# Norm and gate of the delta rule's outputs for both token tiles ahead of one pause, then all transposes

## The chip, the cores and the metric

The kernel runs on one core of one Trainium2 chip. The metric is the device time of one execution in microseconds (us). The profiler also records one execution as a trace; its times below are given from the start of the profiled span. Engines: PE multiplies and transposes, with its weight loads (PEld) beside it; DVE is the vector engine, ACT the scalar engine, POOL is GpSimd, and SP issues most of the transfers.

## The reference, cut to what matters

The layer is a normed mixer with two branches over 256 tokens of width 2048. Both branches read one combined projection of the normed input. Branch A is a gated delta rule with 8 heads of 128, branch B a causal attention with 8 heads of 128. Each branch is gated with a SiLU path, projected to 2048 and merged with sigmoid gates; then come the output projection, a norm and the residual. The change concerns the end of branch A:

```python
def step(state, inp):
    qg_i, kd_i, u_i, w_i, a_i, gl_i = inp
    v_new = u_i - jnp.einsum('bhcd,bhde->bhce', w_i, state)
    o = jnp.einsum('bhcd,bhde->bhce', qg_i, state) + jnp.einsum('bhij,bhje->bhie', a_i, v_new)
    state = state * gl_i[..., None, None] + jnp.einsum('bhcd,bhce->bhde', kd_i, v_new)
    return state, o
...
oa = gated_delta_rule(qa, ka, va, beta, g).transpose(0, 2, 1, 3)
oa = oa * lax.rsqrt(jnp.mean(oa * oa, axis=-1, keepdims=True) + NORM_EPS)
za = gdn_z.astype(jnp.float32).reshape(B, S, GDN_HEADS, GDN_HEAD_DIM)
oa = (oa * gdn_norm_w.astype(jnp.float32) * jax.nn.silu(za)).reshape(B, S, GDN_WIDTH)
u_a = oa @ w_branch_a
```

So each head's 128 outputs of a token are divided by their root mean square, multiplied by a weight and by the SiLU gate `za`, and the result enters a projection.

## The kernel before, in words

The 256 tokens are two token tiles of 128 rows (`NT` = 2). The weights stream through SBUF in blocks of 1 MB (`raw`, three buffers), and each block is split in pieces into a rounded part and the rest: ACT casts `hi` (L214) and DVE subtracts to get `lo` (L215), three buffers each. PE multiplies `hi` and `lo` with the split input `hT` in three or two matmuls per 128 rows of weight (`proj_n`, `proj_t`, all through the helper at L140). The list `ORDER` (L40) sets the order of these weight blocks: `mk0` is the first block of attention queries and keys (tiles `a_mq`, `a_mk`), after it come `mk1` and then `gb0`, the first block of the second merge gate (tile `a_gb`).

Everything else is written between those matmuls. Each side job is a Python generator in a `Queue` (L45). `tick()` (L132) is called after every fourth `hi`/`lo` pair of `proj_t` and after every six matmuls of `proj_n`; it takes 0.5 off a queue's pause, and when the pause is used up it runs the generator to its next `yield`, whose value is the new pause. The queue `gq` holds the delta rule: its scores, the triangular inverse (`inverse`, L598) and `solve` (L695). The queues `aq` hold the attention heads (`attend`, L805), one queue for even and one for odd heads. Matmuls and transposes are pinned to the order in which they are written (L137), so on PE a transpose that is not ready holds up every matmul behind it. ACT and DVE also take their instructions in order; for them a scheduler may move unpinned instructions past each other.

`solve` first forms the new values in seven steps (`sv`, L700 to L729). Then `outputs(t)` (L731) does for each token tile: the products of the two groups of four heads (`so`, L740 to L743), the squares and their sums on ACT (`jo`, L747), the factor of the norm (`fo`, L751 to L758, with a square root on ACT), and per group the gating on DVE (`os`, L763, four instructions of one head each), a pause of `OS_WAIT` = 5 (L771), four transposes on PE (`ot`, L774), and the split of the result into `oT` on ACT (L779) and DVE (L780). The tiles `os` come from the pool `wk` with two buffers under the tag "s", which the attention's scores `s` also use.

PSUM has four banks for projections (`acc`) and four for everything else (`aux`); `so`, `ot`, the attention's scores `ms`, transposed weights `pp`, products `po` and transposed results `pt` all take the latter in turn.

Two tiles reuse the buffers of the delta rule: `obT`, where the attention heads put their results, and `gb`. Whoever asks for one of them first empties the queue, so that nothing is left that still reads the old contents:

```python
def free_tile(shape, dtype, tag, name):
    gq.drain()
    return big.tile(shape, dtype, tag=tag, name=name)
```

An attention head asks for `obT` at its end (L841), after its pauses `A_WAIT2` = 6, `A_WAIT3` = 3 and `A_WAIT4` = 4 and behind its transposes `pt`. The gate `zg` of the delta rule lies in the buffer "z2", into which POOL later loads a block of the output weights (`tq`, L903). The buffers "tv" and "tw" hold the triangular inverse, and much later sums of the output product (L892).

Of the kernel before, what the change touches and what calls it, by code (L numbers as in the profile page):

```python
# [8 lines left out]
F32 = mybir.dt.float32  # L9
# [6 lines left out]
P = 128  # L16
# [16 lines left out]
OS_WAIT = 5  # L33
# [39 lines left out]
def hybrid_layer(  # L73
# [17 lines left out]
    NT = S // P  # L91
# [19 lines left out]
    big = ctx.enter_context(tc.tile_pool(name="big", bufs=1))  # L111
    wraw = ctx.enter_context(tc.tile_pool(name="wraw", bufs=3))
    wspl = ctx.enter_context(tc.tile_pool(name="wspl", bufs=3))
    wk = ctx.enter_context(tc.tile_pool(name="wk", bufs=2))
# [7 lines left out]
    def aux_tile(name):  # L122
        return aux.tile([P, 512], F32, tag="aux", name=name)
# [15 lines left out]
    def mm(*args, **kwargs):  # L139
        return pin(nc.tensor.matmul(*args, **kwargs))  # L140

    def tr(*args):
        return pin(nc.tensor.transpose(*args))
# [26 lines left out]
    ident = cst.tile([P, P], F32, name="ident")  # L170
# [298 lines left out]
    HG = H // 2  # L469
# [6 lines left out]
    def sl(h):  # L476
        return gsl[h // HG][:, h % HG, :]

    def vt(t, h):
        return gvt[h // HG][:, t, h % HG, :]  # L480
# [100 lines left out]
    def queries(p):  # L581
        h = 2 * p
        pq = proj_t(CQ + h * P, f"q{h}")
        qTs = [halves(pq[m], f"q{h + m}") for m in range(2)]
        for m in range(2):
            conv_silu(qTs[m], h + m)
        for m in range(2):
            gq.add(scores(h + m, kTs[p][m], qTs[m]))
        if p == H // 2 - 1:
            gq.add(inverse())  # L590
            gq.add(solve())
# [103 lines left out]
    def solve():  # L695
        oT = big.tile([P, H, 2 * S], F32R, tag="u1", name="oaT")
        oaT[0] = oT
        lo_, hi_ = slice(0, 64), slice(64, 128)

        def step(t, which):  # L700
            for g in range(2):
                ps = aux_tile(f"sv_{t}_{which}_{g}")
                p3 = ps.rearrange("p (h e) -> p h e", e=P)
                for hh in range(4):
                    h = g * 4 + hh
                    o_ = slice(hh * P, (hh + 1) * P)
                    if which == 0:
                        mm(ps[lo_, o_], inv[0][lo_, t, h, :], vt(t, h)[lo_], start=True, stop=True)
                    elif which == 1:
                        mm(  # L710
                            ps[hi_, o_],
                            sl(h)[lo_, t * 4 * P + 64 : t * 4 * P + 128],
                            vt(t, h)[lo_],
                            start=True,
                            stop=True,
                        )
                    elif which == 2:
                        mm(ps[hi_, o_], inv[0][hi_, t, h, :], vt(t, h)[hi_], start=True, stop=True)
                    else:
                        mm(ps[:, o_], sl(h)[:, P : 2 * P], vt(0, h), start=True, stop=True)  # L720
                v_ = gvt[g][:, t]
                if which == 0:
                    nc.scalar.copy(v_[lo_], p3[lo_])
                elif which == 1:
                    nc.vector.tensor_tensor(v_[hi_], v_[hi_], p3[hi_], op=ALU.subtract)
                elif which == 2:
                    nc.scalar.copy(v_[hi_], p3[hi_])
                else:
                    nc.vector.tensor_tensor(gvt[g][:, 1], gvt[g][:, 1], p3, op=ALU.subtract)  # L729

        def outputs(t):  # L731
            pso = []
            for g in range(2):
                ps = aux_tile(f"so_{t}_{g}")
                pso.append(ps)
                for hh in range(4):
                    h = g * 4 + hh
                    o_ = slice(hh * P, (hh + 1) * P)
                    if t == 0:
                        mm(ps[:, o_], sl(h)[:, 2 * P : 3 * P], vt(0, h), start=True, stop=True)  # L740
                    else:
                        mm(ps[:, o_], sl(h)[:, 3 * P : 4 * P], vt(0, h), start=True, stop=False)
                        mm(ps[:, o_], sl(h)[:, 5 * P : 6 * P], vt(1, h), start=False, stop=True)  # L743
                for hh in range(4):
                    h = g * 4 + hh
                    jq = wk.tile([P, P], BF16, tag="jq", name=f"jo_{t}_{h}")
                    nc.scalar.activation(  # L747
                        jq, ps[:, hh * P : (hh + 1) * P], AF.Square, accum_out=ssoo[:, t, h : h + 1]
                    )
                yield 0.5  # L750
            nc.vector.tensor_scalar(  # L751
                fo[:, t, :], ssq[:, t, :], EPS, EPS * P, op0=ALU.add, op1=ALU.mult
            )
            nc.vector.scalar_tensor_tensor(
                fo[:, t, :], ssoo[:, t, :], 1.0 / P, fo[:, t, :], op0=ALU.mult, op1=ALU.add
            )
            nc.scalar.activation(fo[:, t, :], fo[:, t, :], AF.Sqrt)
            nc.vector.reciprocal(fo[:, t, :], fo[:, t, :])  # L758
            for g in range(2):
                os_ = wk.tile([P, 4, P], F32, tag="s", name=f"os_{t}_{g}")  # L760
                for hh in range(4):
                    h = g * 4 + hh
                    nc.vector.scalar_tensor_tensor(  # L763
                        os_[:, hh, :],
                        pso[g][:, hh * P : (hh + 1) * P],
                        fo[:, t, h : h + 1],
                        zg()[:, t, h * P : (h + 1) * P],
                        op0=ALU.mult,
                        op1=ALU.mult,
                    )  # L770
                yield OS_WAIT  # L771
                pt = aux_tile(f"ot_{t}_{g}")
                for hh in range(4):
                    tr(pt[:, hh * P : (hh + 1) * P], os_[:, hh, :], ident)  # L774
                p3 = pt.rearrange("p (h n) -> p h n", n=P)
                hi = oT[:, g * 4 : g * 4 + 4, t * P : (t + 1) * P]
                lo = oT[:, g * 4 : g * 4 + 4, S + t * P : S + (t + 1) * P]
                gn = pcol[:, NTAP * NCV : NTAP * NCV + 1]
                nc.scalar.activation(hi, p3, AF.Copy, scale=gn)  # L779
                nc.vector.scalar_tensor_tensor(  # L780
                    lo, p3, gn, hi.bitcast(F32), op0=ALU.mult, op1=ALU.subtract
                )
                yield 0.5

        while vq.items or v_left[0]:
            yield 1
        for t in range(NT):
            for which in range(3):
                step(t, which)
                yield SV_WAIT  # L790
            if t == 0:
                step(0, 3)
                yield SV_WAIT
        for t in range(NT):
            yield from outputs(t)

    mv = big.tile([P, NT, GW], F32, tag="z1", name="mv")

# [320 lines left out]
```

## Time and profile before

| | before |
|---|---|
| median of 3 runs | 786.91 us (785.95 to 787.24) |
| the profiled execution | 785.26 us |
| its span, first to last instruction | 783.2 us |
| PE busy in the span | 770.5 us |
| DVE busy | 530.8 us |
| ACT busy | 412.1 us |
| mean granted TensorE clock | 0.994 |

In a line of the page or of a group, "L140 PE MATMUL so<-gdn" names the source line, the engine, the operation and the tiles written and read; a helper's line stands for all who call it, so the tiles tell which step it is. A bracket at the end of a line gives how long the engine stood idle before it and what ended that. Ends of matmuls are modelled and overlap; starts are what can be compared. An fp32 product or a chain of two counts each of its matmuls.

### The profile page before, as it was taken

What the parts mean: (1) busy time and instruction counts of PE and PEld (TensorE: products, weight loads), DVE (VectorE), ACT (ScalarE), POOL (GpSimd) and SP (SyncE); (2) the same over time, 40 slices, a digit from 0 to 9 for tenths busy, and PEclk for the clock granted to TensorE, in tenths of its full rate; (3) what the DMA queues carried; (4) which work ended last, traced back from release to release, by engine and by line L of the source; (5) the groups of instructions that cost most, each with busy time, mean ns of one, the idle gap of its engine ahead of it and who ended that gap; (6) DMA issues with size and microseconds to landing.
All of it is one profiled execution on the core that took longest, in us unless ns stands there. A gap on an engine that the chain in (4) does not pass through costs nothing.

```text
span 783.2 us, 10310 instructions
## 1 busy us (share of the span) xinstructions
PE 770.5 (98%) x3947; PEld 657.4 (84%) x3947; DVE 530.8 (68%) x876; ACT 412.1 (53%) x623; POOL 24.6 (3%) x47
## 2 busy tenths in 40 slices
PE   8999999999999999999999989999999999999996
PEld 7898988898888888888888878888888888888884
DVE  5777668887865898975444646554645668986573
ACT  5676666565554545455536546455464445465551
POOL 3000000010020000001100000000000000000000
PEclk9999999999999999999999999999999999999998
DMA  8576675466578656556833454556456555577442
GB/s 306 165 235 213 189 208 166 148 194 191 166 227 266 210 167 211 181 198 201 229 108 108 162 161 162 168 163 206 164 166 226 201 181 205 194 279 269 163 159 108
DMA packets 92823, 149.24 MB, mean 191 GB/s; under 512 B 3045, under 2 KB 46694, under 8 KB 92134
## 3 DMA queue, kind: packets, MB, share of 16 engines
q1 hardware_dynamic: 89958, 136.51, 54.1%
q0 software_dynamic: 2240, 11.02, 4.8%
q10 hardware_dynamic: 576, 1.05, 0.4%
q8 instruction: 31, 0.51, 0.3%
q14 instruction: 18, 0.15, 0.1%
HBM read 145.42 MB, written 3.15 MB: 190 GB/s over the span
## 4 chain that ended last, share of the span: by engine, by line
PE 95%; DVE 2%; ACT 2%; DMA 1%; issue 0%; SPq 0%; DVEq 0%; ACTq 0%
PE a_gb L140 11%; PE a_ga L140 11%; PE a_y L140 11%; PE a_zg L140 6%; PE a_mq L140 6%; PE a_mk L140 6%; PE a_v L140 6%; PE a_k L140 6%; PE a_zm L140 6%; PE a_mv L140 5%; PE a_ub L140 5%; PE a_ua L140 5%; PE a_q L140 4%; PE sv L140 2%; PE s L140 1%; PE so L140 1%
## 5 line engine op out<-in xcount | busy, mean ns | idle before, releaser
L140 PE MATMUL a_gb<-hi_gb,hT 128*128 128x512 f32 x256 | 83.4, 398 | 0.0
L140 PE MATMUL a_ga<-hi_ga,hT 128*128 128x512 f32 x256 | 80.8, 391 | 0.0
L215 DVE TENSOR_TENSOR lo_gb<-raw_gb,hi_gb 128x1024 fp32r<-128x1024 f32 x32 | 39.1, 1224 | 42.2 <-ACT hi_gb L214 42.2
L214 ACT CAST hi_gb<-raw_gb 128x1024 fp32r<-128x1024 f32 x32 | 33.7, 1052 | 51.2 <-PE a_gb L140 35.7
L140 PEld LDWEIGHTS a_gb<-hi_gb,hT 128*128 128x128 f32 x256 | 48.5, 189 | 10.0
L140 PEld LDWEIGHTS a_ga<-hi_ga,hT 128*128 128x128 f32 x256 | 48.1, 188 | 9.9
L214 ACT CAST hi_ga<-raw_ga 128x1024 fp32r<-128x1024 f32 x32 | 33.6, 1052 | 37.9 <-PE a_ga L140 28.0
L215 DVE TENSOR_TENSOR lo_ga<-raw_ga,hi_ga 128x1024 fp32r<-128x1024 f32 x32 | 39.1, 1223 | 16.6 <-ACT hi_ga L214 16.3
L140 PE MATMUL a_gb<-lo_gb,hT 128*128 128x512 f32 x128 | 50.1, 391 | 0.0
L140 PE MATMUL a_ga<-lo_ga,hT 128*128 128x512 f32 x128 | 49.9, 390 | 0.0
L140 PE MATMUL a_zg<-hi_zg,hT 128*128 128x348 f32 (+1 forms) x192 | 46.6, 322 | 0.0
L140 PE MATMUL a_mq<-hT,hi_mq 128*128 128x512 f32 x128 | 46.4, 405 | 0.0
L140 PE MATMUL a_mk<-hT,hi_mk 128*128 128x512 f32 x128 | 46.1, 402 | 0.0
L140 PE MATMUL a_y<-hi_y,mT 128*128 128x512 f32 x144 | 45.7, 390 | 0.0
L140 PE MATMUL a_v<-hT,hi_v 128*128 128x512 f32 x128 | 45.6, 399 | 0.0
L140 PE MATMUL a_q<-hT,hi_q 128*128 128x512 f32 x128 | 45.3, 395 | 0.0
L140 PE MATMUL a_ua<-hi_ua,oaT 128*128 128x512 f32 x128 | 41.8, 395 | 0.0
L140 PE MATMUL a_k<-hT,hi_k 128*128 128x512 f32 x128 | 40.7, 400 | 0.0
L140 PE MATMUL a_zm<-hi_zm,hT 128*128 128x512 f32 x128 | 40.6, 392 | 0.0
L140 PE MATMUL a_mv<-hi_mv,hT 128*128 128x512 f32 x128 | 40.1, 391 | 0.0
L140 PE MATMUL a_ub<-hi_ub,obT 128*128 128x512 f32 x128 | 40.1, 389 | 0.0
L140 PE MATMUL a_v<-hT,lo_v 128*128 128x256 f32 x128 | 35.9, 281 | 0.0
(318 smaller groups left out, 1909.6 us busy)
## 6 DMA issues: line engine op xcount, KB each, us to landing
raw_ga<-in_w_in_dram SPq DMA_DIRECT2D x16, 1024.0 KB, 5.1
raw_gb<-in_w_in_dram SPq DMA_DIRECT2D x16, 1024.0 KB, 5.0
raw_y<-in_w_out_dram SPq DMA_DIRECT2D x15, 1024.0 KB, 5.0
raw_q<-in_w_in_dram SPq DMA_DIRECT2D x8, 1024.0 KB, 5.5
raw_mv<-in_w_in_dram SPq DMA_DIRECT2D x8, 1024.0 KB, 5.1
raw_v<-in_w_in_dram SPq DMA_DIRECT2D x8, 1024.0 KB, 5.7
raw_zm<-in_w_in_dram SPq DMA_DIRECT2D x8, 1024.0 KB, 9.0
raw_mq<-in_w_in_dram SPq DMA_DIRECT2D x8, 1024.0 KB, 5.7
```

Source lines behind the costliest of these rows:

```text
L140: return pin(nc.tensor.matmul(*args, **kwargs))
L214: nc.scalar.copy(hi, raw)
L215: nc.vector.tensor_tensor(lo, raw, hi.bitcast(F32), op=ALU.subtract)
```

## The change

`outputs` is divided in two. `normed(t, oz)` does the products, the squares, the factor and the gating of one token tile, with a yield of 0.5 where the pause of 5 was, and writes the gated outputs into a tile `oz` of its own. `turned_outputs(t, oz)` does the transposes and the split. `solve` runs `normed` for both token tiles, then pauses once for `OS_WAIT`, then runs `turned_outputs` for both. The two `oz` tiles, 4 KB per partition each, take the buffers "tv" and "tw"; the tiles `os` are gone.

```diff
-        def outputs(t):
+        def normed(t, oz):
             pso = []
 ...
             for g in range(2):
-                os_ = wk.tile([P, 4, P], F32, tag="s", name=f"os_{t}_{g}")
                 for hh in range(4):
                     h = g * 4 + hh
                     nc.vector.scalar_tensor_tensor(
-                        os_[:, hh, :],
+                        oz[:, g, hh, :],
                         pso[g][:, hh * P : (hh + 1) * P],
                         fo[:, t, h : h + 1],
                         zg()[:, t, h * P : (h + 1) * P],
                         op0=ALU.mult,
                         op1=ALU.mult,
                     )
-                yield OS_WAIT
+                yield 0.5
+
+        def turned_outputs(t, oz):
+            for g in range(2):
                 pt = aux_tile(f"ot_{t}_{g}")
                 for hh in range(4):
-                    tr(pt[:, hh * P : (hh + 1) * P], os_[:, hh, :], ident)
+                    tr(pt[:, hh * P : (hh + 1) * P], oz[:, g, hh, :], ident)
 ...
-        for t in range(NT):
-            yield from outputs(t)
+        ozs = [big.tile([P, 2, HG, P], F32, tag=tg, name=f"oz_{t}") for t, tg in enumerate(("tv", "tw"))]
+        for t in range(NT):
+            yield from normed(t, ozs[t])
+        yield OS_WAIT
+        for t in range(NT):
+            yield from turned_outputs(t, ozs[t])
```

## The prediction

> **What bounds the kernel now.** I read the page first, then PE's waits, then the chain around the changed lines, then the instructions in order of time there. The page says that TensorE sets the time:
>
> ```profile
> span 783.2 us, 10310 instructions
> PE 770.5 (98%) x3947; PEld 657.4 (84%) x3947; DVE 530.8 (68%) x876; ACT 412.1 (53%) x623; POOL 24.6 (3%) x47
> PE 95%; DVE 2%; ACT 2%; DMA 1%; issue 0%; SPq 0%; DVEq 0%; ACTq 0%
> ```
>
> PE carries 95% of the chain that ended last, so an edit can only pay where PE stands still. PE's list of waits has three entries in the whole span (total, times, longest):
>
> ```profile
> PE ot L143 <- DVE os L763: 2.4, 1, 2.4
> PE hTp L143 <- DMA x<-in_x_dram: 1.4, 2, 0.9
> PE warm L140 <- DVE epst L174: 1.1, 1, 1.1
> ```
>
> The longest lies in the changed function: the transposes `ot` wait for the gating `os`. The chain there (start, us, what) leaves PE and goes through the squares on ACT and the gating on DVE:
>
> ```profile
> 465.58 1.80 PE so L140 x16
> ...
> 467.47 1.14 ACT jo L747 x8
> ...
> 469.47 0.36 DVE os L763
> ...
> 469.97 2.19 PE ot L143 x8
> ```
>
> Why does it happen there and only there? `obT` reuses the buffer of the delta rule's data, so the first finished attention head calls `gq.drain()` (L681), which writes out everything left of `outputs` at once, without the pauses. From its first `so` product, `outputs` needs per token tile 0.5+0.5+5+0.5+5+0.5 = 12 units of pause, 24 for both, and a tick takes 0.5 off: the last transposes are due 47 ticks after the first `so`. The attention head was issued a tick earlier and has 6+3+4 = 13 units = 26 ticks to its tail, so the drain comes at tick 25. By then tile 0 is through, and tile 1 issues its second `so` in that same tick (12.5 units); its squares, `fo`, eight gatings and eight transposes all stand in one knot, with PE's transposes in program order behind them.
>
> **The knot's price.** PE in order of time:
>
> ```profile
> 443.58 0.60 PE L143 MATMUL ot<-ident,os 128*128 128x128 f32 x4
> 443.93 0.48 PE L140 MATMUL a_gb<-hi_gb,hT 128*128 128x512 f32 x1
> 444.25 0.40 PE L140 MATMUL a_gb<-lo_gb,hT 128*128 128x512 f32 x1
> 444.48 0.63 PE L140 MATMUL a_gb<-hi_gb,hT 128*128 128x512 f32 x2
> ...
> 462.26 1.95 PE L140 MATMUL so<-gdn 128*128 128x128 f32 x16
> 463.96 0.48 PE L140 MATMUL a_gb<-hi_gb,hT 128*128 128x512 f32 x1
> ...
> 465.42 1.95 PE L140 MATMUL so<-gdn 128*128 128x128 f32 x16
> 467.20 0.38 PE L143 MATMUL pt<-ident,om 128*128 128x128 f32 x2
> 469.97 2.19 PE L143 MATMUL ot<-ident,os 128*128 128x128 f32 x8 [2.38 <-DVE os L763]
> 471.96 0.63 PE L143 MATMUL pt<-ident,om 128*128 128x128 f32 x2
> 472.24 0.77 PE L140 MATMUL a_gb<-hi_gb,hT 128*128 128x512 f32 x1
> 472.81 0.63 PE L140 MATMUL a_gb<-lo_gb,hT 128*128 128x512 f32 x1
> 473.24 0.96 PE L140 MATMUL a_gb<-hi_gb,hT 128*128 128x512 f32 x2
> 474.04 0.39 PE L140 MATMUL a_gb<-lo_gb,hT 128*128 128x512 f32 x1
> 474.27 0.62 PE L140 MATMUL a_gb<-hi_gb,hT 128*128 128x512 f32 x2
> ```
>
> Ends are modelled, so I count from start to start. Undisturbed, one `so` group takes 463.96-462.26 = 1.70 us, four transposes 443.93-443.58 = 0.35, a projection matmul 444.48-444.25 = 0.23, and the first one after an inserted group 444.25-443.93 = 0.32, so an insertion costs 0.09 beside its own work. From 465.42 to 474.27 PE does one `so` group (1.70), eight `ot` (0.70), four `pt` (0.35) and five projection matmuls (5 x 0.23 + 0.09 = 1.24): 3.99 us of work in 8.85 us. The knot costs 4.86 us, twice the wait in the list.
>
> The rest of it has two sources. The transposes run at the gatings' pace. And the granted clock falls (window, us, PE busy with count, clock, DMA share, GB/s):
>
> ```profile
> 470.50:471.00 0.50, 0.50 (x2) 0.56 0.00 0
> ...
> 473.50:474.00 0.50, 0.50 (x2) 0.53 0.43 115
> 474.00:474.50 0.50, 0.50 (x3) 1.00 0.49 90
> ```
>
> About 3.4 us at half clock. At full clock the last `ot` would still follow the last gating (469.47 + 2.16 = 471.63, row below); with about 0.1 for it, 0.18 for two `pt` and 1.24 for the five matmuls PE would stand at 474.27's place by 473.2. So 1.1 us of the 4.86 is the half clock and 3.8 is waiting.
>
> Here a rule can be weighed. The Trainium skill, "TensorE: Matmul & The Clock Gate", section "HAM oscillation — how this bites in real kernels", says that gaps of PE up to about 3.4 us leave the clock alone. The row shows a 2.38 us wait followed by half clock, so the trace disagrees on the gap's length, while the 3.4 us at half clock agree with the length of the window that the page states. By the page's rule the knot would have cost 3.8 us, not 4.86.
>
> **The change part by part.** *Pauses.* In the new order the first two `so` groups stay, the third comes 4 ticks after the first, the fourth 5; one pause of 5 follows and the transposes go out one group per tick. Total 2+2+5+2 = 11 units; the last transpose is due at tick 21, four ahead of the drain at 25. In the changed program's PE order four ticks of `a_gb` indeed lie between the last `ot` and `pt`. The drain finds nothing: gain 4.86 us.
>
> *PE work.* The same 24 products and 16 transposes. Groups put between projection matmuls: before `ot`, `ot`, `so`, and the knot (counted above) make 4; after, `so`, `so`, four `ot` and one with both `pt` make 7. Three more at 0.09 = 0.27 us. Bounds: 0, if they merged, and 7 x 0.09 = 0.63; I take 0.27, counted from the order.
>
> *Gatings and squares moved up.* No instruction is added; ACT's table loads stay in number and place. They come between the splits of the `mk` and `gb` weights, on queues that run in order. Rows of that stretch, of PE, DVE and ACT in order of time:
>
> ```profile
> 431.62 0.40 PE L140 MATMUL a_mk<-hT,hi_mk 128*128 128x512 f32 x1
> ...
> 434.44 0.40 PE L140 MATMUL a_mk<-hT,hi_mk 128*128 128x512 f32 x1
> ```
>
> ```profile
> 431.86 0.20 DVE L758 RECIPROCAL fo<-fo 128x8 f32<-128x8 f32 x1 [0.30 <-ACT fo L757]
> ...
> 438.44 1.22 DVE L215 TENSOR_TENSOR lo_gb<-raw_gb,hi_gb 128x1024 fp32r<-128x1024 f32 x1 [1.60 <-ACT hi_gb L214]
> ...
> 469.47 2.16 DVE L763 SCALAR_TENSOR_TENSOR os<-so,fo,zg 128x128 f32<-128x128 f32 x8
> ```
>
> ```profile
> 434.52 1.05 ACT L214 CAST hi_mk<-raw_mk 128x1024 fp32r<-128x1024 f32 x1 [1.38 <-PE a_mk L140]
> ```
>
> Eight pairs of `a_mk` take 434.44-431.62 = 2.82 us. Two `so` groups (3.4 us) now stand in that PE stream, from 431.62 on, so PE reaches each later weight about 3.5 us later, the last `mk` group at 431.62 + 3.5 + 3 x 2.82 = 443.6, the first `gb` after another 2.82 and six transposes of the scores (6 x 0.09) at 447.1. Against it: tile 0's gatings take DVE from 432.1 to 434.2. Tile 1's second `so` group ends on PE near 436.5; four squares on ACT (1.14 us, the chain's row) end near 437.7; then come the last `mk` cast (its buffer is free from 438.0), done at 439.2, its difference on DVE, 440.4, and only then tile 1's `fo` and eight gatings, 442.8. Behind them waits the first `lo_gb`, done at 444.0 and needed at 447.3: 3.3 us to spare. The `mk` difference has 443.6-440.4 = 3.2. So they are hidden by PE's own added work; without that cover they would cost up to 2.2 us each tile.
>
> *PSUM.* The third `so` takes the bank of a score product that DVE has read before tile 0's squares; the last two `ot` take the banks of `po`, freed by DVE gatings `om` some ticks earlier. Price 0; at worst one gating pair, 0.6 us.
>
> *Tiles.* The new tiles take the slots of the triangular inverse, whose last user is done before the first `sv` product; nothing is queued there until the sums much later. POOL's first weight load into the gate's slot is freed 30 us earlier:
>
> ```profile
> 472.23 0.79 POOL L903 DMA_DIRECT2D tq<-in_w_out_dram x1 [97.47 <-ACT oaT L779]
> ```
>
> One transfer of 1 MB moves from 472 to about 443, beside weight loads that are issued two buffers ahead of PE. No cast in this stretch waits for a DMA (the cast in the row above was released by PE). Price 0; at worst a late weight load, which is no more than the 3.3 us bound above again.
>
> *What is late next.* Right after the knot ACT is the busiest engine but PE (window; columns: length, then PE, PEld, DVE and ACT busy):
>
> ```profile
> 475.00:485.00 10.00, 10.00 (x56) 8.66 (x55) 6.35 (x13) 9.02 (x16) 0.00 (x0) 1.00 0.57 188
> ```
>
> ACT is busy 9.02 of 10 us. PE is full there all the same, and ACT's casts and sigmoids are released by PE, so they move forward with it. The sum: 4.86 - 0.27 = 4.6 us. The profiled execution took 785.26 us (span 783.2), below the median of the runs shown, 786.91; it would become 780.7. Taken off the median: **782.3 us**.
>
> **The rivals.** *The half clock is not in every run.* If the timed runs waited but kept the clock, the gain is 3.8 - 0.27 = 3.5 us: 783.4. For: the gap is short and the mean over runs is not traced. Against: the one trace shows it. *The gain is given back.* The knot let ACT, DVE and DMA run ahead by 4.9 us; if the stage after it hung on ACT (9.02 of 10), PE would wait there: 786.9. Against: no later PE wait in the list, and ACT there waits for PE. The same time would come if the drain still found the transposes, which the new order excludes. *Slower:* the gatings starve the splits between 436 and 447. The first `lo_gb` has 3.3 us to spare; the loss begins beyond that and eats the gain at 3.3 + 4.6 = 7.9 us late. At 10 us, which needs each of the 16 gatings to take 0.6 us longer than its 0.27, the result is 789.0. The row of eight gatings at 2.16 us speaks against it.
>
> **How the numbers follow.** Forecast 782.3: 0.70. Clock kept: 0.18. Given back: 0.07. Starved: 0.05. The range takes in the first two, 0.88 together, with the bounds of the insertions (0 and 0.63 for 0.27) and the spread of the runs shown, 1.29 us (785.95 to 787.24), as the error of the level: low 782.3 - 0.27 - 1.3 = 780.7, high 783.4 + 0.36 + 1.3 = 785.0 rounded. 0.2% of this kernel is 1.6 us, about what a measurement of it can tell; both first cases pass it: faster 0.88, same 0.07, slower 0.05.
>
> **What would show it.** In the changed trace PE's list has only the two waits at the start; no window between 420 and 500 has a clock under 1.00; `oz` gatings stand at about 432 and 441, `ot` at about 457 to 462, `pt` pairs at about 468 in one group; PE reaches the next heads' first `ms` about 4.6 us earlier than before. The forecast is wrong if a new PE wait on `lo_mk`, `lo_gb` or `lo_mq` appears, or if the span from there to the end has grown.

## The result, and the profile after

The changed kernel took 780.94 us in the median (780.70 to 781.96, 4 runs), the kernel before 786.96 us (785.95 to 787.24, 4 runs): a ratio of 0.9928, 95% interval 0.9911 to 0.9945. Run again later beside more runs of the kernel before, it took 781.12 us against 785.98 us, ratio 0.9932 (0.9918 to 0.9947), so the gain is about 5 us. The profiled execution took 780.75 us, its span 778.8 us, 4.4 us less than before.

The page of the changed kernel, its totals and the chain's shares by engine:

```profile
span 778.8 us, 10308 instructions
PE 768.0 (99%) x3947; PEld 655.4 (84%) x3947; DVE 530.7 (68%) x876; ACT 412.1 (53%) x623; POOL 24.6 (3%) x47
PE 95%; DVE 2%; ACT 2%; DMA 1%; issue 0%; SPq 0%; DVEq 0%
```

The work is the same: DVE and ACT are busy as long as before to 0.1 us. PE's busy time fell by 2.5 us, although it does the same products and transposes; 2.3 us of that lie in the stretch that is compared below, where the transposes went at the gatings' pace and what followed ran at half clock. The list of what PE waited for (total, times, longest):

```profile
PE hTp L143 <- DMA x<-in_x_dram: 1.7, 2, 1.1
PE warm L140 <- DVE epst L174: 1.1, 1, 1.1
PE a_k L140 <- ACT hi_k L267: 0.2, 1, 0.2
```

The wait of `ot` for the gating is not in it any more. All three that are left lie in the first ten microseconds. PE in order of time, the side jobs around the change (start, us, what):

```profile
431.92 1.95 PE L140 MATMUL so<-gdn 128*128 128x128 f32 x16
435.12 1.95 PE L140 MATMUL so<-gdn 128*128 128x128 f32 x16
...
456.83 0.60 PE L143 MATMUL ot<-ident,oz 128*128 128x128 f32 x4
458.67 0.60 PE L143 MATMUL ot<-ident,oz 128*128 128x128 f32 x4
460.50 0.60 PE L143 MATMUL ot<-ident,oz 128*128 128x128 f32 x4
462.33 0.60 PE L143 MATMUL ot<-ident,oz 128*128 128x128 f32 x4
468.26 0.60 PE L143 MATMUL pt<-ident,om 128*128 128x128 f32 x4
472.84 1.47 PE L140 MATMUL ms<-y_mk,y_mq 128*128 128x128 f32 x8
```

The four groups of transposes follow each other by one tick and are all out 6 us before `pt`, where the drain comes. PE is busy there throughout and the clock stays at 1.00 (window, us, busy time and count of PE, PEld, DVE, ACT and POOL, clock, DMA share, GB/s):

```profile
460.00:470.00 10.00, 10.00 (x51) 8.25 (x50) 6.43 (x9) 5.08 (x7) 0.00 (x0) 1.00 0.59 157
470.00:480.00 10.00, 10.00 (x55) 8.60 (x54) 5.99 (x14) 8.71 (x16) 0.00 (x0) 1.00 0.52 159
```

DVE at the same time shows the gatings between the weight splits:

```profile
432.40 2.16 DVE L763 SCALAR_TENSOR_TENSOR oz<-so,fo,zg 128x128 f32<-128x128 f32 x8
...
440.83 2.16 DVE L763 SCALAR_TENSOR_TENSOR oz<-so,fo,zg 128x128 f32<-128x128 f32 x8
442.90 1.22 DVE L215 TENSOR_TENSOR lo_gb<-raw_gb,hi_gb 128x1024 fp32r<-128x1024 f32 x1
```

For comparing kernels I use one stretch of PE's stream: from the first heads' score products `ms`, a tick before the first `so`, to the next heads' `ms`, behind the drain. Everything that the change moves on PE lies in it. In the kernel before it runs from 421.50 to 477.25:

```profile
421.50 1.47 PE L140 MATMUL ms<-y_mk,y_mq 128*128 128x128 f32 x8
...
477.25 1.47 PE L140 MATMUL ms<-y_mk,y_mq 128*128 128x128 f32 x8
```

That is 55.75 us. In the changed kernel it is 472.84 - 421.80 = 51.04 us. The gain in it is 4.71 us. What follows it to the end of the span is as long in both: 783.2 - 477.25 = 305.95 and 778.8 - 472.84 = 305.96 us. So nothing of the gain was given back later; the span itself fell by 0.3 us less than the stretch because this execution reached the stretch at 421.80 instead of 421.50.

| kernel | median us | before, run beside it | ratio (95%) | stretch us |
|---|---|---|---|---|
| changed, first runs | 780.94 | 786.96 | 0.9928 (0.9911 to 0.9945) | 51.04 |
| changed, again | 781.12 | 785.98 | 0.9932 (0.9918 to 0.9947) | 51.04 |
| own tiles alone | 786.27 | 785.98 | 0.9998 (0.9987 to 1.001) | 55.74 |
| own tiles, pauses of 2 | 781.54 | 785.98 | 0.9941 (0.9928 to 0.9955) | 51.14 |
| changed, pause of 9 | 781.33 | 785.98 | 0.9939 (0.9926 to 0.9952) | 51.33 |
| changed, second tile late | 785.46 | 786.06 | 0.9991 (0.998 to 1.0001) | 55.57 |
| before, PE kept busy | 784.65 | 786.06 | 0.9984 (0.9973 to 0.9994) | 54.70 |
| changed, gating x4 | 787.39 | 786.06 | 1.0013 (1.0003 to 1.0024) | 56.86 |
| changed, gating x2 | 780.72 | 786.06 | 0.9933 (0.9916 to 0.9951) | 51.04 |

### The profile page after: what moved, and what is told of

It reads as the page before. It is cut to its first block, busy times and chain, and to the rows that moved or that the text cites. A ratio compares the mean times of both kernels' runs of the same rounds, so it can differ in the third digit from the quotient of the medians.

```text
span 778.8 us, 10308 instructions
## 1 busy us (share of the span) xinstructions
PE 768.0 (99%) x3947; PEld 655.4 (84%) x3947; DVE 530.7 (68%) x876; ACT 412.1 (53%) x623; POOL 24.6 (3%) x47
## 3 DMA queue, kind: packets, MB, share of 16 engines
q10 hardware_dynamic: 576, 1.05, 0.4%
## 4 chain that ended last, share of the span: by engine, by line
PE 95%; DVE 2%; ACT 2%; DMA 1%; issue 0%; SPq 0%; DVEq 0%
PE a_gb L140 11%; PE a_ga L140 11%; PE a_y L140 11%; PE a_k L140 6%; PE a_zg L140 6%; PE a_mq L140 6%; PE a_mk L140 6%; PE a_v L140 6%; PE a_zm L140 6%; PE a_mv L140 5%; PE a_ub L140 5%; PE a_ua L140 5%; PE a_q L140 4%; PE sv L140 2%; PE s L140 1%; PE po L140 1%
```

## The experiments

The theory: the loss was one knot, the second token tile's chain exposed behind the drain, with half clock after it. The rival: the change pays through its parts as such, the tiles of their own, the work in one go, or the single pause.

**The changed kernel again.**

> The changed kernel itself, to narrow the gain. The knot theory (squares, factor, gating and transposes of the second token tile stood in one chain behind the emptied queue; 4.86 us of PE time, less 0.27 for three more insertions) expects 4.6 us under the kernel before. The medians shown so far differ by 6.0 us; if that stays, some 1.4 us come from outside the changed stretch or from a knot that costs more in other executions than in the traced one.

Measured: 4.9 us between the medians, 4.71 us in the stretch. The larger difference of the first medians did not stay, and its interval had held 4.6 us already.

**One part alone: tiles of their own.**

```diff
-                os_ = wk.tile([P, 4, P], F32, tag="s", name=f"os_{t}_{g}")
+                os_ = oz[:, g]
```

with `oz` in the buffers "tv" and "tw" as in the change, pauses and order as before.

> The kernel before with one part of the change alone: the gated outputs go into tiles of their own (buffers tv and tw), the pauses and the order stay. Knot theory: the second token tile is still issued at the drain, the wait of PE for the gating stays at about 2.4 us with half clock behind it, and the time stays at the kernel before, within 0.5 us. Rival (the buffers that the gated tiles shared with the attention's scores were what cost): 4 to 6 us faster.

Measured: no change (ratio 0.9998), and the wait is back to the same tenth:

```profile
PE ot L143 <- DVE oz L763: 2.4, 1, 2.4
```

The granted clock there, in the columns used above:

```profile
470.00:471.00 1.00, 0.21 (x2) 0.18 (x2) 0.96 (x5) 0.00 (x0) 0.00 (x0) 1.00 0.00 0
471.00:472.00 1.00, 1.00 (x5) 0.61 (x5) 1.00 (x5) 0.01 (x1) 0.00 (x0) 0.68 0.00 0
472.00:473.00 1.00, 1.00 (x6) 0.85 (x6) 0.74 (x3) 0.68 (x1) 0.00 (x0) 0.50 0.00 0
473.00:474.00 1.00, 1.00 (x4) 0.87 (x4) 0.72 (x2) 0.95 (x2) 0.79 (x1) 0.50 0.06 16
474.00:475.00 1.00, 1.00 (x4) 0.80 (x3) 0.82 (x2) 0.00 (x0) 0.00 (x0) 0.61 0.57 70
```

The shared buffers cost nothing by themselves: with own tiles the first gatings ran at 432.92, ahead of `pp`, and not at 442.40 behind it (each in its own trace), and nothing was gained. By the program's order they do forbid short pauses: a gated tile must wait until `pp` has read the scores from its buffer, and on PE a transpose `ot` written ahead of `pp` would wait for work behind itself. This is argued from the order; a short pause with shared tiles was not run.

**The same order, only earlier.**

```diff
-OS_WAIT = 5
+OS_WAIT = 2
```

on top of the own tiles; each group of four heads is still gated, paused and turned one after the other.

> Own tiles and the order of the kernel before (each group of four heads gated, paused, turned), but a pause of 2 for each group instead of 5, so that the last transposes are due at tick 23, ahead of the drain at 25. Knot theory: no wait of PE, no half clock, 4.3 to 4.9 us faster than the kernel before, as with the change, though nothing is done in one go. Rival (it is the one pause for all and the gating in one go that pays): at most half of that gain.

Measured: 51.14 us in the stretch and a ratio of 0.9941, the whole gain to 0.1 us, though nothing is done in one go. PE has no wait in the stretch, and the last transposes are out 3.2 us ahead of `pt`:

```profile
466.33 0.60 PE L143 MATMUL ot<-ident,oz 128*128 128x128 f32 x4
...
469.55 0.60 PE L143 MATMUL pt<-ident,om 128*128 128x128 f32 x4
```

So it is not the batching that pays, but that the last group is out before the drain. Here the first `ot` stands ahead of `pp` (435.88 and 443.82), which by the argument above needs own tiles.

**Transposes pushed into the drain.**

```diff
-OS_WAIT = 5
+OS_WAIT = 9
```

in the changed kernel.

> The changed kernel with the one pause at 9 instead of 5: no transpose is due before the drain at tick 25, so all sixteen are written out there, after products, squares and gating that are long done. Knot theory: the drain costs nothing when its data is ready; no wait of PE, and four insertions fewer at 0.09 us, so 0.3 to 0.4 us faster than the change, about 5.0 us under the kernel before. Rival (work pushed out by the drain costs by itself): the wait of PE is back and 2 to 5 us of the gain are lost.

Measured: the gain stays (0.9939), so the drain does not cost when its data is ready. The 0.3 to 0.4 us for fewer insertions did not come; the stretch is 0.29 us longer. PE there:

```profile
466.99 0.38 PE L143 MATMUL pt<-ident,om 128*128 128x128 f32 x2
467.21 1.98 PE L143 MATMUL ot<-ident,oz 128*128 128x128 f32 x16
469.38 0.44 PE L143 MATMUL pt<-ident,om 128*128 128x128 f32 x2 [0.19 <-DVE oaT L783]
469.57 0.48 PE L140 MATMUL a_gb<-hi_gb,hT 128*128 128x512 f32 x1
```

Twenty transposes take 469.57 - 466.99 = 2.58 us; at 0.35 for four, as in the prediction, they would take 1.75. Six PSUM tiles in a row (`pt`, four `ot`, `pt`) want more than the four banks, and each bank must be read by ACT and DVE before it is used again (the bracket names DVE's read). That 0.83 us is more than the four insertions save.

**The second tile late again, in the changed kernel.**

```diff
             yield from normed(t, ozs[t])
+            if t == 0:
+                yield 10
         yield OS_WAIT
```

> The changed kernel with a pause of 10 between the first and the second token tile, so that the second tile's last product falls on the drain as in the kernel before; tiles of their own and the order 'all gating, then all transposes' stay. Knot theory: squares, factor, gating and transposes of the second tile are exposed again; the first tile's eight transposes (0.7 us) run inside the wait and two separate insertions (0.09 us each) fall away, so about 0.9 us less than the kernel before, near 785.1 us, with a wait of PE for the gating of 1.5 to 2 us. Rival (own tiles, one pause, gating in one go are what pays): as the change, 781.1 us.

Measured: 785.46 us, a stretch of 55.57 us; nearly the whole knot is back with own tiles, one pause and all gating ahead of all transposes. The expected 0.9 us under the kernel before was 0.2 in the stretch:

```profile
466.60 0.60 PE L143 MATMUL ot<-ident,oz 128*128 128x128 f32 x4
469.28 2.94 PE L143 MATMUL ot<-ident,oz 128*128 128x128 f32 x12 [2.08 <-DVE oaT L783]
472.01 0.63 PE L143 MATMUL pt<-ident,om 128*128 128x128 f32 x2
```

Only four of the first tile's eight transposes ran ahead of the wait. The wait ends with DVE's read of the bank that these four had filled, and DVE had to wait for ACT's half of the same split, which stood behind the second tile's squares (on ACT from 466.64):

```profile
467.74 0.70 ACT L782 ACTIVATE oaT<-ot,pcol 128x512 fp32r<-128x512 f32 x1
468.47 0.75 DVE L783 SCALAR_TENSOR_TENSOR oaT<-ot,pcol,oaT 128x512 fp32r<-128x512 f32 x1 [0.41 <-ACT oaT L782]
```

The half clock is back too:

```profile
470.00:471.00 1.00, 1.00 (x5) 0.61 (x5) 1.00 (x5) 0.66 (x1) 0.00 (x0) 0.67 0.00 0
471.00:472.00 1.00, 1.00 (x5) 0.77 (x5) 1.00 (x4) 0.69 (x1) 0.00 (x0) 0.50 0.00 0
```

**The kernel before with PE kept busy in the drain.** This kernel does ten extra products that nobody reads:

```diff
             tr(pt[:, t * P : (t + 1) * P], om[:, t, :], ident)
+        if h == 0:
+            keep_busy = acc_tile("keep_busy")
+            for i in range(10):
+                mm(keep_busy[:, :P], ones, ones, start=True, stop=True)
         obT = ob_tile()
```

> The kernel before with ten products of 128x128 on constants (about 2.1 us, into a free accumulator bank, nobody reads them) put on PE right behind the first head's transposes, where PE stood idle in the drain. The chain on ACT and DVE is left as it is. Clock part of the knot theory: the half clock of 3.4 us came from that idle time; it goes, the wait for the gating shrinks to about 0.3 us, and the time falls by 1.1 us, to about 784.9 us (stretch from one pair of score products to the next 54.6 instead of 55.75 us). Rival (the clock falls for another reason, or the slow matmuls after the wait are slow anyway): half clock still there, 55.75 us.

Measured: the stretch is 476.18 - 421.48 = 54.70 us, 1.05 us shorter with 2.4 us more work in it, and the median follows (784.65 against 786.06). PE, and the clock by windows:

```profile
467.40 2.40 PE L140 MATMUL keep_busy<-ones 128*128 128x128 f32 x20
469.94 2.05 PE L143 MATMUL ot<-ident,os 128*128 128x128 f32 x8
471.82 0.38 PE L143 MATMUL pt<-ident,om 128*128 128x128 f32 x2
```

```profile
470.00:471.00 1.00, 0.98 (x5) 0.52 (x5) 1.00 (x5) 0.01 (x1) 0.00 (x0) 1.00 0.00 0
471.00:472.00 1.00, 1.00 (x7) 0.70 (x7) 0.89 (x4) 0.68 (x1) 0.00 (x0) 1.00 0.09 16
472.00:473.00 1.00, 1.00 (x7) 0.82 (x6) 0.72 (x2) 0.95 (x2) 0.78 (x1) 1.00 0.00 0
```

The chain on ACT and DVE still ends at the same place (the transposes start at 469.94, before at 469.97), but there is no half clock. So the half clock was a consequence of the idle time and cost 1.05 us, and the waiting cost the rest.

**The cover of the moved gatings.** In the changed kernel the second tile's gatings are written several times, with the same values:

```diff
-                for hh in range(4):
+                for hh in [hh for hh in range(4) for _ in range(4 if t == 1 else 1)]:
```

> The changed kernel with each gating of the second token tile done four times (same values, 24 more DVE instructions of 0.27 us, 6.5 us, ahead of the first lo_gb). Cover theory: the first lo_gb was done at 444.1 us and PE needed it at about 447.4; it now comes near 452 us, PE waits for it 4 to 5 us, and the clock falls to half behind that wait: 5 to 6.5 us slower than the change, near 787 us. Rival (the cover is much larger than 3.3 us, or the scheduler's order hides it): as the change.

Measured: 56.86 us in the stretch, 5.8 us more than the change, and 787.39 us. PE's wait (list of waits), PE in order of time, and the clock behind it:

```profile
PE a_gb L140 <- DVE lo_gb L215: 4.0, 1, 4.0
```

```profile
446.97 0.39 PE L140 MATMUL a_gb<-hi_gb,hT 128*128 128x512 f32 x1
451.39 0.80 PE L140 MATMUL a_gb<-lo_gb,hT 128*128 128x512 f32 x1 [4.03 <-DVE lo_gb L215]
```

```profile
450.00:452.00 2.00, 0.61 (x2) 0.52 (x3) 2.00 (x3) 0.00 (x0) 0.79 (x1) 0.81 0.04 8
452.00:454.00 2.00, 2.00 (x6) 1.62 (x5) 1.60 (x2) 0.00 (x0) 0.00 (x0) 0.50 0.86 270
```

This is the slower rival of the prediction, made to happen: the late `lo_gb` stops PE and brings half clock with it. From start to start the stop costs 451.39 - 446.97 - 0.23 = 4.19 us; the other 1.6 us of the 5.8 fit 3.4 us at half clock.

With `2 if t == 1` in the same line:

> The same with each gating of the second token tile done twice (8 more, 2.2 us). Cover theory: the first lo_gb is 1 to 2.2 us later, still ahead of PE's need, so no wait and the time of the change within 0.4 us. Rival (DVE is already at its limit in this stretch): 1 to 2 us slower.

Measured: 51.04 us in the stretch, 780.72 us, no wait. DVE in order of time:

```profile
441.26 3.45 DVE L763 SCALAR_TENSOR_TENSOR oz<-so,fo,zg 128x128 f32<-128x128 f32 x13
444.62 1.22 DVE L215 TENSOR_TENSOR lo_gb<-raw_gb,hi_gb 128x1024 fp32r<-128x1024 f32 x1
```

Three of the sixteen gatings came behind the first `lo_gb`: thirteen stood ahead of it instead of eight. Counted from the first `ms` of the stretch, since the executions reach it at different times (422.23 here), it started at 22.39 us instead of 21.10, 1.3 us later. That hides. With the gating four times (first `ms` at 421.48) it started at 28.64, 7.5 us later:

```profile
450.12 2.36 DVE L215 TENSOR_TENSOR lo_gb<-raw_gb,hi_gb 128x1024 fp32r<-128x1024 f32 x2
```

The edge between the two was not measured.

## Why the prediction was right

*The knot and its place.* Right. The wait, its cause (the drain at tick 25) and its end are as described: own tiles alone leave it, having the second tile out before the drain removes it in both orders that were run, and putting the second tile's products back on the drain brings it back.

*Its price.* 4.86 us were counted from start to start, twice the 2.4 us in the list of waits. With 0.27 us for insertions the sum was 4.6; the stretch gave 4.71. The terms were good to about 0.1 us; which of them holds the rest was not measured.

*The split of that price.* Half clock 1.1 us, waiting 3.8. With PE kept busy the stretch lost 1.05 us. The rival in which the timed runs keep the clock can be weighed by the mean granted clock of each timed run: of the 29 runs of the kernel before that stand beside the last experiments, 25 have 0.995 or less, three 0.996 and one 0.998; the ten runs of the changed kernel and the twelve with PE kept busy have 0.996 to 0.998. 3.4 us at half clock make 0.002 of the mean over 783 us. So nearly all runs of the kernel before had it, as far as a mean can tell; the one at 0.998 took 784.02 us, 2.0 us under their median, and the two of the twelve runs with own tiles alone that had 0.998 took 783.79 and 783.94 us. On the weighed rule: the Trainium skill, "TensorE: Matmul & The Clock Gate", section "HAM oscillation — how this bites in real kernels", warns of idle gaps of PE over about 3.4 us, which the prediction took to mean that shorter ones leave the clock alone. Waits of 2.1 us (second tile late) and 2.4 us (own tiles alone) were each followed by half clock, so for the wait alone the traces disagree with that reading. But these waits lie between transposes, and what those do to the clock was not separated (see the last section).

*Insertions.* Three more at 0.09 us; the starts of the changed trace give 0.11 for one (one `ot` and six matmuls 458.67 - 456.83 = 1.84 us, of which 0.35 and 6 x 0.23 are the work, which leaves 0.11).

*Moved gatings.* Forecast at 432.1 and about 440.6 to 442.8, first `lo_gb` done at 444.0 and needed at 447.3; they ran at 432.40 and 440.83, and it was done at 442.90 + 1.22 = 444.12, in a trace that reaches the stretch 0.30 us later. In the changed trace PE uses it here:

```profile
447.52 0.39 PE L140 MATMUL a_gb<-lo_gb,hT 128*128 128x512 f32 x1
```

That leaves 3.4 us, forecast 3.3, and the two gating experiments stand on its two sides. The price beyond this room was set too low: by the prediction's rule a `lo_gb` 7.5 us late costs 7.5 - 3.3 = 4.2 us, which is the stop that was measured, but the half clock behind it was left out, and the whole loss was 5.8 us.

*Nothing given back.* Right: 305.95 and 305.96 us behind the stretch.

*The level.* The forecast of 782.3 us was 1.4 us above the median. In those first runs the kernel before stood at 786.96, near the level assumed, so the difference shows there as a gain of 6.0 instead of 4.6 us. Beside the later and more numerous runs of the kernel before (785.98 us) the gain is 4.9 us; 4.6 taken off that level gives 781.4, against 781.12. So most of the error is the level of three runs and not a step, and the 1.3 us that the range allowed for it were needed.

## What to carry to other kernels

A wait in the list of waits is not its price: count from start to start between two marks of the bounding engine, since pacing and the clock behind the wait can double it. Where a queue is emptied by force because a buffer is wanted back, look at which half-finished chain it catches; here it was enough to have that chain's steps out some ticks earlier, and the number of pauses or tiles did not matter by itself. Asking for the buffer later was not run. Work moved off an exposed chain needs room where it lands: here the next weight split had 3.4 us of it, and starting it 7.5 us later turned the gain into a loss.

## What the runs showed of the hardware that was not expected

Half clock came after waits of PE as short as 2.08 us and lasted 3.4 us each time. In windows of 0.1 us it began 0.6 us after PE was working again in the kernel before and with own tiles alone, 1.1 us after with the second tile late, and 0.2 us before PE's next matmul with the gating four times. In the first three, transposes stand on both sides of the wait. From the start of the first transpose to the half clock it was 3.4 us (kernel before, 467.20 to 470.56), 3.3 us (own tiles alone) and 4.0 us (second tile late); with the gating four times it was 4.0 us from the end of PE's last matmul (446.97 + 0.23). So two readings fit these traces: a wait of about 2 us is enough, or the clock falls after some 3.3 us without a product or a projection matmul, and transposes do not count. No run here has a wait of 2 us between projection matmuls, which would tell them apart.

Filling the wait with products that nobody reads made the kernel faster (54.70 against 55.75 us).

Executions of one kernel reach the first `ms` of the stretch at different times, 421.48 to 422.94 us over ten traces, while the stretch of the changed kernel is 51.04 us in both of its traces; so differences between single executions here come mostly from before the stretch, and a stretch between two marks compares kernels better than the whole span. Where before it they arise was not followed.
